# Half-length rows for the second tile's loads and the first store in an fp32 interleave kernel

## The chip, the cores and the metric

The kernel runs on 1 core of one Trainium2 chip. The metric is the device time of one execution in microseconds (us). I call the two versions "the kernel before" and "the changed kernel". The span in a profile runs from the first to the last instruction that the profile shows. Spans are compared with spans and times with times.

## The reference

```python
# x, y: (32, 256, 1024) float32
result = np.zeros((32, 256, 2048), dtype=np.float32)
result[..., 0::2] = x
result[..., 1::2] = y
```

It is pure data movement: 67.1 MB are read and 67.1 MB written.

## The kernel before

Inputs and output are taken as flat arrays. Eight tiles of 128 partitions x 8192 elements are loaded from x and from y, so a partition's row is 32 KiB. VectorE interleaves each tile in two halves into an output tile of 128 x 8192, whose row is 32 KiB as well. Loads are issued from SyncE (queue q1), stores from ScalarE (queue q10). x, y and output tiles have two buffers each.

```python
WL = 8192; WS = 4096
xpool = ...(name="xp", bufs=2); ypool = ...(name="yp", bufs=2); opool = ...(name="op", bufs=2)
...
nc.scalar.dma_start(out=first, in_=zero)      # a small store of zeros at the very start
for lw in lwidths:                            # 8 tiles
    ...
    nc.sync.dma_start(out=xtile, in_=xs)
    nc.sync.dma_start(out=ytile, in_=ys)
    while soff < lw:                          # 2 halves
        otile = opool.tile([P, 2 * WS], fp32, name="otile")
        ...
        nc.vector.tensor_copy(out=otile[:, 0::2], in_=xsub)
        nc.vector.tensor_copy(out=otile[:, 1::2], in_=ysub)
        nc.scalar.dma_start(out=os_, in_=otile)
```

## Time and profile before

| what | value | from |
|---|---|---|
| time, median of the first 3 runs | 316.41 us (315.72 to 316.87) | runs |
| span of the profiled run, whose time is 315.62 us | 313.8 us | page, first line; runs |
| VectorE busy | 23% | page, part 1 |
| both DMA queues together | 99.4% of the 16 engines' time | page, part 3 |
| moved | 428 GB/s over the span, 433 from 31 to 311 us | page; stretches |

The page is read from the DMA parts. The share of a queue says how long its packets took, as a part of 16 engines times the span. Two shares that add up to almost 100% leave no room for any gain but shorter or fewer packets. Numbers are taken from the packet records (start, length and size of every row that an engine moved). The text of the prediction shows the other views.

### The profile page before, as it was taken

Reading aid. Unit: us, or ns where it says so; the run is one execution under the profiler, and the core shown is the slowest. Engines: PE = TensorE matmul, PEld = TensorE weight load, DVE = VectorE, ACT = ScalarE, POOL = GpSimd, SP = SyncE. Lnnn points to the kernel's source line nnn. Section 1 sums busy time; section 2 is a strip of 40 time slices with the busy share of each in tenths; the row PEclk is TensorE's granted clock in tenths of the full one; section 3 lists DMA queues with packets and bytes.
Section 4 is the critical chain, followed back from the end, with each engine's and each line's share of the span. In section 5 each row is a group of like instructions: output and inputs, shape, how many; then the busy total and the mean of one; then the engine's idle time right before and its main releaser. Section 6 shows DMA issues by size and latency. Waiting matters only on the chain.

```text
span 313.8 us, 152 instructions
## 1 busy us (share of the span) xinstructions
DVE 72.8 (23%) x33; POOL 0.2 (0%) x4
## 2 busy tenths in 40 slices
DVE  0433002231032410325003150130501305023500
POOL 0000000000000000000000000000000000000000
DMA  8999999999999999999999999999999999999997
GB/s 339 464 405 397 468 401 464 405 464 405 464 405 464 405 459 409 451 418 451 418 434 434 430 439 426 443 413 455 401 468 401 468 401 468 401 468 401 464 405 334
DMA packets 4640, 134.23 MB, mean 428 GB/s; under 512 B 528, under 2 KB 544, under 8 KB 544
## 3 DMA queue, kind: packets, MB, share of 16 engines
q1 hardware_dynamic: 2304, 67.11, 49.9%
q10 hardware_dynamic: 2336, 67.12, 49.5%
HBM read 67.11 MB, written 67.12 MB: 428 GB/s over the span
## 4 chain that ended last, share of the span: by engine, by line
DMA 83%; DVE 11%; DVEq 1%; issue 0%
DMA out_dram<-otile 76%; DMA ytile<-in_y_dram 7%; DVE otile L71 6%; DVE otile L70 5%; DVEq L83 1%; DVEq L70 0%
## 5 line engine op out<-in xcount | busy, mean ns | idle before, releaser
L70 DVE COPY otile<-xtile 128x4096 f32<-128x4096 f32 x16 | 36.6, 2295 | 184.9 <-DMA out_dram<-otile 173.7
L71 DVE COPY otile<-ytile 128x4096 f32<-128x4096 f32 x16 | 36.6, 2292 | 39.8 <-DMA ytile<-in_y_dram 39.8
L45 DVE MEMSET zero<- 16x128 f32 x1 | 0.2, 165 | 0.9 <-PEq L119 0.9
L119 POOL MEMSET const-bfloat16-1.0<- 128x1 bf16 x1 | 0.1, 102 | 0.0
L119 POOL MEMSET const-uint8-127<- 128x1 uint8 x1 | 0.1, 102 | 0.0
L119 POOL MEMSET const-float32-0.0<- 128x1 f32 x1 | 0.1, 99 | 0.2 <-issue 0.2
L119 POOL MEMSET const-float32-1.0<- 128x1 f32 x1 | 0.1, 99 | 0.0
## 6 DMA issues: line engine op xcount, KB each, us to landing
out_dram<-otile ACTq DMA_DIRECT2D x16, 4096.0 KB, 29.1
xtile<-in_x_dram SPq DMA_DIRECT2D x8, 4096.0 KB, 43.6
ytile<-in_y_dram SPq DMA_DIRECT2D x8, 4096.0 KB, 60.7
out_dram<-zero ACTq DMA_DIRECT2D x1, 8.0 KB, 6.3
```

Source lines behind the costliest of these rows:

```text
L45: nc.vector.memset(zero, 0.0)
L70: nc.vector.tensor_copy(out=otile[:, 0::2], in_=xsub)
L71: nc.vector.tensor_copy(out=otile[:, 1::2], in_=ysub)
L83: tc.compile()
L119: nc = _bacc.Bacc("TRN2", target_bir_lowering=False, num_devices=1)
```

## The change

The second tile's x and y loads, and the first store, are each issued as two transfers of half a row (16 KiB) in every partition. Bytes and copies stay the same. The intent that I read from it is to let the first tiles get moving in smaller steps: the first copies of tile two need only the first halves, and a queue that gets the engine for one row at a time holds it for a shorter time. (The cut below is shortened; its last call is broken over fewer lines than in the kernel.)

```diff
-        nc.sync.dma_start(out=xtile, in_=xs)
-        nc.sync.dma_start(out=ytile, in_=ys)
+        parts = 2 if start == P * lw else 1
+        for t, s in ((xtile, xs), (ytile, ys)):
+            step = lw // parts
+            for c in range(0, lw, step):
+                nc.sync.dma_start(
+                    out=t[:, c : c + step],
+                    in_=dataclasses.replace(s, offset=start + c, ap=[[lw, P], [1, step]]),
+                )
...
-            nc.scalar.dma_start(out=os_, in_=otile)
+            step = width if start == 0 and soff == 0 else 2 * width
+            for c in range(0, 2 * width, step):
+                nc.scalar.dma_start(
+                    out=dataclasses.replace(os_, offset=2 * start + 2 * soff + c,
+                                            ap=[[2 * lw, P], [1, step]]),
+                    in_=otile[:, c : c + step],
+                )
```

More of the change, by code (lines that the diff above doesn't have):

```diff
@@ L71, in _interleave @@
             nc.vector.tensor_copy(out=otile[:, 1::2], in_=ysub)
-            nc.scalar.dma_start(out=os_, in_=otile)
+            step = width if start == 0 and soff == 0 else 2 * width
+            for c in range(0, 2 * width, step):
+                nc.scalar.dma_start(
+                    out=dataclasses.replace(
+                        os_,
+                        offset=2 * start + 2 * soff + c,
+                        ap=[[2 * lw, P], [1, step]],
+                    ),
+                    in_=otile[:, c : c + step],
+                )
             soff += width
```

## The prediction

> **What bounds the kernel now.** I read the page's header, its DMA parts and its chain first, because the kernel does no arithmetic: it reads 67.11 MB, interleaves, and writes 67.12 MB.
>
> ```profile
> span 313.8 us, 152 instructions
> DVE 72.8 (23%) x33; POOL 0.2 (0%) x4
> ...
> DMA packets 4640, 134.23 MB, mean 428 GB/s; under 512 B 528, under 2 KB 544, under 8 KB 544
> q1 hardware_dynamic: 2304, 67.11, 49.9%
> q10 hardware_dynamic: 2336, 67.12, 49.5%
> ...
> DMA 83%; DVE 11%; DVEq 1%; issue 0%
> ```
>
> The two queues (q1 the loads, q10 the stores) together fill 99.4% of the 16 engines' time. Of q1's 2304 packets, 256 are 4-byte completions (16 for each of 16 loads), so 2048 are rows of 32 KiB, 128 on each engine; q10 has as many. 49.9% of 313.8 is 156.6 us, or 1.223 us a row; 49.5% is 155.3 us, or 1.213 us a row. In the packet records nearly every row takes exactly 1.213 us. So the floor is 256 rows per engine x 1.213 = 310.5 us, only 3.3 us (1.05%) under the span. VectorE, at 23%, is no bound.
>
> Next, where those 3.3 us are. I asked for stretches of the span (columns: DVE and POOL busy, clock, DMA share, GB/s):
>
> ```profile
> 1.00:22.00 21.00, 4.53 (x4) 0.00 (x0) 1.00 1.01 423
> 24.00:31.00 7.00, 2.50 (x2) 0.00 (x0) 1.00 0.97 379
> 31.00:311.00 280.00, 63.61 (x28) 0.00 (x0) 1.00 1.00 433
> ```
>
> From 31 to 311 us nothing is lost: 433 GB/s for 280 us. The losses are three. The start: the first row begins at 0.99 us, and first rows take about 2.0 us in place of 1.213 (together about 1.7 us). The entry of the stores: the 16 load rows that begin near 27.3 us, just ahead of the first store rows, take 1.69 to 1.88 us, about 0.57 us too long on every engine. The end: the last row ends near 312.7 us and the last store lands at about 313.1, about 1 us for the landing and the closing. Only the second lies in what the change touches.
>
> Third, the waits and the tail, because the change moves when buffers come free:
>
> ```profile
> DVE otile L70 <- DMA out_dram<-otile: 173.7, 14, 21.6
> DVE otile L71 <- DMA ytile<-in_y_dram: 39.8, 8, 5.2
> DVE otile L70 <- DMA xtile<-in_x_dram: 11.3, 1, 11.3
> ```
>
> ```profile
> 287.67 2.29 DVE L71 COPY otile<-ytile 128x4096 f32<-128x4096 f32 x1 [4.92 <-DMA ytile<-in_y_dram]
> 290.00 8.66 ACTq L72 DMA_DIRECT2D out_dram<-otile  x2
> 293.80 2.30 DVE L70 COPY otile<-xtile 128x4096 f32<-128x4096 f32 x1 [3.83 <-DMA out_dram<-otile]
> ```
>
> VectorE's 225 us of waiting is for DMA that is itself busy: consequences, not costs. The tail matters. The last load lands at 287.65 us. The store then in flight lands at 293.70, so 6.05 us, that is 5 rows, of it are left. In those 5 rows VectorE copies the last y (2.29 us), the next store is issued at 290.00, and the engines never run dry.
>
> **What the Trainium skill says.** The page "DMA: Bandwidth & Descriptors", section "Queues, rings and completion order", says that each engine round-robins between the queues with work, a packet at a time. The trace agrees, with one 32 KiB row as the turn: from 30 us on the packet records show 16 load rows, 16 store rows, in strict alternation. So a queue's share goes by the size of its rows, and this is the lever of the change. The same page, section "Where 436 GB/s comes from", puts the ceiling at 435 GB/s; the trace shows 433, so there is 0.5% of head room. Its section "Why small descriptors are slow (HBM only)" charges a fixed overhead per packet. The records let me size it: 27 ns for a 512-byte row and 1213 ns for 32 KiB, a line with 1186 / 32256 ns per byte and about 8 ns fixed. "Perfetto Trace Analysis", section "DMA Optimizations", says that splitting lets some transfers start sooner if the DMA engines are generally idle; here they are not.
>
> **The change, part by part.** The instruction order shows the same copies on VectorE, four loads of half rows in place of two for the second tile (x first half, x second, y first, y second), two half-row stores in place of the first one, and nothing else but which completion semaphores are shared.
>
> 1. *Rows.* Two loads and one store get 256 half rows each in place of 128 rows: 384 more packets, 24 per engine. By the line above a half row takes 0.61 us, so 24 x 8 ns = 0.2 us, on the bound. Three more completions per engine at 9 ns are 0.03 us. Sum: +0.2 us.
>
> 2. *Entry of the stores.* The first store is issued at 24.32 us and its first rows begin at 29.10: 4.8 us, in which load rows already taken up by the engines run out. If the engines hold a count of rows, half rows shorten this toward 2.4 us, and may halve the 0.57 us of slow load rows. I take -0.3 us, the only term that can gain. The earlier start itself gains nothing, as loads fill the engines anyway.
>
> 3. *The lead of the loads over the stores.* Before, it settles near 21 rows and stays, as both queues alternate row for row. While the first store (half rows) meets the second tile (half rows), shares stay equal: after 8 rows of store, about 29 of load are done (28 if the stores enter earlier), with 3 to 4 rows of y left. Then the second store has full rows against half rows and gets two thirds: it moves 6 to 8 rows while the loads move 3 to 4. The lead falls to 17 or 18 rows. From then on rows are equal again.
>
> 4. *What the smaller lead does.* Each even store (the first half of a tile) needs its y landed. With lead 21, 5 rows of the odd store are left at that moment, and between loads and stores they last 12 us (94.05 to 106.20 us in the timeline). With lead 18, 2 rows are left, lasting 4 x 1.213 = 4.9 us; the copy takes 2.3 us and the entry of a store up to 4.8, together 7.1. The store queue would run dry for about 2 us. But loads are queued behind, so the engines don't stop: they do 2 more load rows, and the lead climbs to some 19 or 20 by itself. Cost: perhaps one more slow entry of 0.57 us, which I count half: +0.3 us.
>
> 5. *Tail.* With lead 19 to 20, 3 to 4 rows (3.6 to 4.9 us) of the last odd store remain when the last y lands. Copy 2.3 us plus issue and start of about 1.0 us (first load: issued at 0.00, first row at 0.99) is 3.3, so little or nothing is lost. With lead 17 it would be 3.3 + 0.8 of a slow first row - 1.2 = 2.9 us. Weighing these, +0.3 us.
>
> 6. *Other waits.* The second half of y1 shares a semaphore with the small zero store, landed by 7.4 us; the third y load now waits for the first half store, landing near 37 us by my reckoning, while some 7 rows of loads are still queued. Both hidden: 0. The y split lets the first copy of tile two start without all of y1, which takes away a wait of 4.9 us at 55.32 us on VectorE; hidden as well: 0.
>
> Sum: 0.2 - 0.3 + 0.3 + 0.3 = +0.5 us on 316.4, which gives 316.9 us.
>
> **The rivals.** *The tail opens:* the lead doesn't recover and the engines stand still before the last two stores. For it: the 2:1 share is a plain consequence of turns by rows. Against: loads stay queued behind, which restores the lead. It would make 318 to 320 us. *The entry becomes smooth:* half rows remove the slow 0.57 us and nothing else happens. For it: the loss sits exactly where the change works. Against: it is all there is to win, and 0.2 us go back in rows. It would make 316.0 us. *Half rows are badly slower than my line,* for instance by 0.1 us each through a change of HBM access: the 48 half rows per engine would cost 5 us, giving 321. Against: 512-byte rows lie on the engine's line, and all big rows take the same 1.213 us for reads and writes. *Nothing but noise:* 316.4 us, within the 1.15 us between the three runs of before.
>
> **Range and chances.** The best case is -0.6 us less noise, about 315.3; the tail at a middling size gives 318.6. Faster by over 2% would need under 310.1 us; the rows alone take 310.5, so this is all but excluded: 1%. Slower by over 2% needs over 322.7 us, more than full tail loss and a second slow entry together: 2%. Within 2%: 97%.
>
> **What would show it.** Right: the DMA share stays near 1.00 from 31 to 311 us; packets rise by 384 + 48 completions; first store rows before 29.1 us and shorter slow rows there; the second store lands sooner than 67.4 us, by about 3 us; at the end the last y lands later and fewer than 5 rows of the store in flight are left. Wrong: a gap in the DMA row near 290 us, half rows that take clearly over 0.61 us, or a lead that stays at 21, which would mean that turns go by bytes rather than rows. The prediction fails if the time is below 315.3 (something hidden in the 280 us was gained) or above 318.6.

## The result, and the profile after

The changed kernel took 316.62 us (median of 6 runs, 316.54 to 316.93), the kernel before beside it 316.15 us (315.67 to 316.87). Ratios here are the mean time of one kernel's fast runs over that of the other's of the same rounds, so not quite the ratio of the medians. This one is 1.0015 (95% interval 1.000 to 1.003): the same at 2%, some 0.5 us longer. The interval reaches 1.000; the repeat in experiment 8 is clear of it (1.0007 to 1.0033).

The page of the changed kernel, in the lines that answer to those of before:

```profile
span 314.5 us, 159 instructions
...
DMA packets 5072, 134.23 MB, mean 427 GB/s; under 512 B 576, under 2 KB 592, under 8 KB 592
q1 hardware_dynamic: 2592, 67.11, 49.9%
q10 hardware_dynamic: 2480, 67.12, 49.5%
```

There are 432 packets more, the 384 half rows and the 48 completions of the working. The shares are what they were: the engines are as full as before, in a span 0.7 us longer (of which some 0.5 us are the fast run that was profiled before). In the packet records a half row takes 611 ns, as worked out.

The stretches of the changed kernel (columns as in the prediction):

```profile
1.00:22.00 21.00, 4.68 (x4) 0.00 (x0) 1.00 1.01 423
24.00:31.00 7.00, 2.34 (x2) 0.00 (x0) 1.00 1.00 382
31.00:311.00 280.00, 63.52 (x28) 0.00 (x0) 1.00 1.00 433
```

The start is equal, the entry of the stores is hardly better (382 GB/s for 379) and the long middle is at 433 GB/s in both. What did move is the order of things. First the timeline of the kernel before from 48 to 70 us, then that of the changed kernel (columns: start, length, engine, line, operation, tiles; in brackets the idle time before it and what ended it):

```profile
48.11 2.29 DVE L70 COPY otile<-xtile 128x4096 f32<-128x4096 f32 x1 [21.62 <-DMA out_dram<-otile]
55.32 2.30 DVE L71 COPY otile<-ytile 128x4096 f32<-128x4096 f32 x1 [4.91 <-DMA ytile<-in_y_dram]
...
67.49 2.30 DVE L70 COPY otile<-xtile 128x4096 f32<-128x4096 f32 x1 [9.88 <-DMA out_dram<-otile]
```

```profile
48.75 2.29 DVE L78 COPY otile<-xtile 128x4096 f32<-128x4096 f32 x1 [22.41 <-DMA out_dram<-otile]
50.95 2.29 DVE L79 COPY otile<-ytile 128x4096 f32<-128x4096 f32 x1
...
65.16 2.30 DVE L78 COPY otile<-xtile 128x4096 f32<-128x4096 f32 x1 [11.92 <-issue]
...
84.69 2.30 DVE L78 COPY otile<-xtile 128x4096 f32<-128x4096 f32 x1 [15.03 <-DMA out_dram<-otile]
97.75 2.29 DVE L79 COPY otile<-ytile 128x4096 f32<-128x4096 f32 x1 [10.77 <-DMA ytile<-in_y_dram]
104.05 2.30 DVE L78 COPY otile<-xtile 128x4096 f32<-128x4096 f32 x1 [4.00 <-DMA out_dram<-otile]
```

The wait for y1 at 55.32 us is gone, and the second store lands 2.3 us sooner: the copy that it releases starts at 65.16 us instead of 67.49. Its full rows met half rows and got about two thirds (71% of the bytes moved from 49.5 to 57 us). The price shows at 97.75 us: the loads are later against the stores, VectorE waits 10.8 us for y (5.0 before), and the next store lands only 4.0 us after that copy (9.9 before).

The end of the changed kernel, to be laid beside the same lines in the prediction:

```profile
290.35 2.30 DVE L79 COPY otile<-ytile 128x4096 f32<-128x4096 f32 x1 [8.74 <-DMA ytile<-in_y_dram]
292.68 6.26 ACTq L82 DMA_DIRECT2D out_dram<-otile  x2
294.07 2.30 DVE L78 COPY otile<-xtile 128x4096 f32<-128x4096 f32 x1 [1.43 <-DMA out_dram<-otile]
```

The last y lands at 290.33 us, 2.7 us later than before, and the store in flight lands at 293.98. So 3.65 us of it are left, where 6.05 were left before. The copy and the start of the next store don't fit into them. The stretch from 292 to 296 us, first before, then changed, shows the hole (second to last column: the DMA share; last: GB/s):

```profile
292.00:296.00 4.00, 2.21 (x1) 0.00 (x0) 1.00 0.93 401
```

```profile
292.00:296.00 4.00, 2.58 (x2) 0.00 (x0) 1.00 0.87 369
```

A short stretch is noisy (in the kernel before the DMA share is 1.48 from 26 to 28 us and 0.61 from 28 to 30), so I also chained the rows of each engine by their ends and starts (the records don't name the engine). In the changed kernel 16 rows end from 293.07 to 293.62 us, and the next 16 start from 293.52 to 293.67: all engines but one stand still, for 0.1 to 0.6 us. In the repeat (experiment 8) up to four go on without a stop.

### The profile page after: what moved, and what is told of

The parts are those of the page before. It is cut to its first block, busy times and chain, and to the rows that moved or that the text cites. A ratio compares the mean times of both kernels' runs of the same rounds, so it can differ in the third digit from the quotient of the medians.

```text
span 314.5 us, 159 instructions
## 1 busy us (share of the span) xinstructions
DVE 72.7 (23%) x33; POOL 0.2 (0%) x4
## 3 DMA queue, kind: packets, MB, share of 16 engines
q10 hardware_dynamic: 2480, 67.12, 49.5%
## 4 chain that ended last, share of the span: by engine, by line
DMA 79%; DVE 11%; issue 4%; DVEq 1%
DMA out_dram<-otile 73%; DMA ytile<-in_y_dram 7%; DVE otile L79 6%; DVE otile L78 5%; DVEq L100 1%; DVEq L78 0%
```

## The experiments

Two theories stood against each other. **Tail theory:** the smaller lead of the loads over the stores opens the hole near 293.6 us, and this is most of the 0.5 us. **Entry theory:** the hole only makes early engines wait for late ones, and what counts is the slowest engine, made later by the half rows themselves and by slow load rows where stores enter the queues (near 27 us). All outputs were correct. Experiments 1 to 4, 5 to 8 and 9 to 11 share their runs of the kernel before (medians 316.22, 315.98 and 315.75 us), and each of these sets ran on a chip of its own (2, 8 and 11); between sets, compare through the kernel before. Neither theory looks outside the DMA; the section on the prediction shows that most of the 0.5 us lies there, and corrects the readings of experiments 1, 5, 6 and 7 for it.

### 1. The second store in half rows too

```diff
-            step = width if start == 0 and soff == 0 else 2 * width
+            step = width if start == 0 else 2 * width
```

> Undoes the unequal share alone: the second store goes in half rows too, so it meets the half rows of y1 on equal terms. Lead theory (the small loss is mostly the tail, through the lead of loads over stores): the second store lands after 67 us as before, the lead stays near 21 rows, about 5 rows (6 us) of the store in flight are left when the last y lands, no gap near 290 us, time 0.3 us over before (the rows and the slow entry), so below the changed kernel. Rival (the loss is the rows and the entry, the tail costs nothing): time 0.5 to 0.6 us over before, no faster than the changed kernel, as there are 8 more rows per engine.

Measured: 316.83 us, ratio 1.0022 (1.0004 to 1.004). The end of its timeline:

```profile
284.76 2.30 DVE L78 COPY otile<-xtile 128x4096 f32<-128x4096 f32 x1 [10.02 <-issue]
286.97 2.29 DVE L79 COPY otile<-ytile 128x4096 f32<-128x4096 f32 x1
289.29 10.03 ACTq L82 DMA_DIRECT2D out_dram<-otile  x2
294.45 2.29 DVE L78 COPY otile<-xtile 128x4096 f32<-128x4096 f32 x1 [5.20 <-DMA out_dram<-otile]
```

The last y landed at 284.68 us, 9.7 us before the store in flight landed. The lead was even over that of before (about 26 rows, not 21): the second store in half rows outlasts y1 and then meets full rows of x2, which I had overlooked. There is no hole, and still the time is not below the changed kernel's. This speaks for the rival, but weakly: the tail theory's 0.3 us over before (a ratio of 1.0009) lies within the interval, and 0.15 us more of its time than of the changed kernel's lie outside the span (table below).

### 2. The first store in half rows, all loads in full rows

```diff
-        parts = 2 if start == P * lw else 1
+        parts = 1
```

> Only the first store in half rows, all loads in full rows. If turns go by rows, the loads get two thirds while the first store runs: it lands near 58 us instead of 48, the lead rises from 21 to about 29 rows, and at the last y some 13 rows (over 12 us) of stores are left, so no tail gap. Time: before plus 0.1 us. If turns go by bytes, the first store lands near 48 us as before. For the entry: if half rows of the store make it slow, the excess near 28 us is over the 0.6 us of before; if it is the loads' rows, it stays at 0.6.

Measured: 316.04 us, ratio 0.9998 (0.998 to 1.0017). The copy that waits for the first store shows when it landed:

```profile
59.30 2.29 DVE L78 COPY otile<-xtile 128x4096 f32<-128x4096 f32 x1 [32.68 <-DMA out_dram<-otile]
```

It landed 11.2 us later than before (59.30 against 48.11), as expected from turns by rows. At the last y, 9.7 us of store were left (landings at 284.34 and 294.02 us), somewhat less than I expected. The slow load rows at the entry came to about 0.95 us per engine, in two rows of each engine, against 0.64 before. The time shows nothing of it. The spans of its runs are even shorter than those of the kernel before (314.17 against 314.52 us on average), but the ranges overlap.

### 3. Only the loads of the second tile in half rows

```diff
-            step = width if start == 0 and soff == 0 else 2 * width
+            step = 2 * width
```

> Only the second tile's loads in half rows. By rows as turns, the first store gets two thirds and lands near 42 us instead of 48. The lead falls to about 16, the store queue runs dry once or twice while loads fill the engines, and the lead comes back to 20 or more by that. Lead theory: if it is back at 20 or more at the end, there is no gap near 290 us, and the time is before plus 0.2 to 0.4 us (rows and entry); if each new entry of the stores costs 0.6 us again, before plus 0.8 to 1.4 us. Rival (lead stays where the start put it): about 0 rows left at the last y, a gap of 3 us, before plus 3 us.

Measured: 317.37 us (median of the five fast runs), ratio 1.0029 (1.0011 to 1.0047); one run of the six, 324.45 us, was slow and is left out of both. That is 0.9 to 1.15 us over before, in the range forecast for the case that each new entry of the stores costs 0.6 us again; but the slow rows after 60 us come to only 0.12 us per engine on average. Its timeline in two places:

```profile
45.40 2.30 DVE L78 COPY otile<-xtile 128x4096 f32<-128x4096 f32 x1 [18.87 <-DMA out_dram<-otile]
...
101.85 2.30 DVE L79 COPY otile<-ytile 128x4096 f32<-128x4096 f32 x1 [13.34 <-DMA ytile<-in_y_dram]
104.06 2.29 DVE L78 COPY otile<-xtile 128x4096 f32<-128x4096 f32 x1
...
289.45 2.29 DVE L79 COPY otile<-ytile 128x4096 f32<-128x4096 f32 x1 [4.88 <-DMA ytile<-in_y_dram]
```

The first store was ahead (45.40 us). At 104.06 us VectorE went on without any wait: the store before had long landed, so the store queue had run dry (no store row runs from 97.6 to 107.7 us). Counted from the packet records the lead was 14.8 rows at 60 us and 21.7 at 120 us. At the last y (289.42 us) 6.1 us of store were left, as before. So the lead comes back by itself, and this kernel has no hole at the end either, but it is the slower one. Its engines end 1.9 us apart (312.54 to 314.48 us; before 312.27 to 312.70), with 8 slow rows between 60 and 284 us, where the kernel before has none. Here, then, a slowest engine does end late.

### 4. Quarter rows in place of half rows

```diff
-        parts = 2 if start == P * lw else 1
+        parts = 4 if start == P * lw else 1
-            step = width if start == 0 and soff == 0 else 2 * width
+            step = width // 2 if start == 0 and soff == 0 else 2 * width
```

> The same change with 8 KiB rows (four parts instead of two), so 4:1 instead of 2:1 against the second store, and 72 extra rows per engine instead of 24. Lead theory with recovery: the lead falls to about 12, the store queue runs dry for some 10 us early on while loads run alone, and the lead jumps to about 22, so the tail has 5 or 6 rows left and no gap: only rows (72 x 5 to 8 ns = 0.4 to 0.6 us) and at most one more slow entry (0.6): before plus 0.5 to 1.2 us. Rival without recovery: the stores end with no rows left at the last y, a gap of 4 us or more, before plus 4 to 5 us.

Measured: 316.91 us, ratio 1.0036 (1.0003 to 1.0068; one run of 319.75 us pulls the mean up). The lead fell to 13.4 rows at 80 us and was 20 to 22 from 120 us on; 4.8 us of store, 4 rows, were left at the last y, one row less than forecast. The recovery that I predicted holds under a disturbance twice as strong, and the cost is in the foreseen range.

### 5 and 6. Half rows for x1 or y1 alone

```diff
+            parts = 2 if start == P * lw and t is xtile else 1     # 5; 6 has: t is ytile
```

> The change with y of the second tile left in full rows: only x1 and the first store are in half rows. x1 is what runs when the first store enters (near 27 us). y1 in full rows meets the half rows of the first store, so loads gain and the tail has over 5 rows left: no tail gap. Entry theory (the half rows of x1 at the entry make the slowest engine later; the first experiment lost its tail gap without getting faster): 0.3 to 0.7 us over before. Tail theory: within 0.2 us of before.

> The change with x of the second tile left in full rows: only y1 and the first store are in half rows. The entry of the stores happens beside full rows of x1, as in the kernel with the store alone. x1 in full rows against the half store lets loads gain about 4 rows, y1 in half rows against the second store loses some: the lead ends near 21 to 24 and the tail has no gap. Entry theory: within 0.2 us of before. Rival (any half rows of loads cost, wherever they run): 0.3 to 0.7 us over before, as with x1 alone.

Measured: x alone 316.23 us, ratio 1.0006 (0.9993 to 1.0019); y alone 316.25 us, ratio 1.0008 (0.9994 to 1.0021). Neither kernel had a hole at the end. The entry theory in its narrow form, that the half rows of x1 running beside the entry do the harm, expected 0.3 us or more for x alone and is not borne out, though the interval (up to 0.6 us) doesn't exclude it. Each costs some 0.2 us, not clear of zero, and none of it lies in the span: the medians of the spans are 314.2 us for both and for the kernel before.

### 7. The hole at the end closed

```diff
-            nc.vector.tensor_copy(out=otile[:, 1::2], in_=ysub)
+            half = width // 2 if start == 7 * P * lw and soff == 0 else width
+            for h in range(0, width, half):
+                nc.vector.tensor_copy(out=otile[:, 2 * h + 1 : 2 * (h + half) : 2],
+                                      in_=ysub[:, h : h + half])
-            step = width if start == 0 and soff == 0 else 2 * width
+            step = width if start in (0, 7 * P * lw) and soff == 0 else 2 * width
```

> The changed kernel, and in the last tile the y copy for its first store and that store in two column halves, so that the store can start 1.15 us earlier after the last y. This closes the gap of about 0.4 us per engine near 293.6 us and touches nothing before 290 us. Tail theory: 0.4 us faster than the changed kernel (0.1 us over before). Entry theory (the gap only lets the earlier engines wait for the later ones, two engines had no gap at all): at most 0.15 us faster than the changed kernel, so 0.3 to 0.5 us over before, with the engines ending more spread than before.

Measured: 316.75 us, ratio 1.0027 (1.001 to 1.0043). The stretch that showed the hole:

```profile
292.00:296.00 4.00, 2.65 (x2) 0.00 (x0) 1.00 0.98 422
```

The hole is closed, and the kernel isn't faster than the changed one in the same rounds (experiment 8). In the chained records the engines now end at 312.58 to 313.20 us, on average 0.27 us sooner than in the changed kernel (312.99 to 313.15), but the last one ends at the same time. So the hole is real, and closing it gains nothing that these runs resolve, where the tail theory had forecast 0.4 us.

### 8. The changed kernel again

> The changed kernel unaltered, beside the three above on the same chip, to see how far its own value moves from one set of rounds to the next. Expected 0.3 to 0.7 us over before; slow load rows at the entry, a gap near 293.6 us in most engines.

Measured: 316.63 us, ratio 1.002 (1.0007 to 1.0033). The changed kernel repeats to 0.01 us in the median; the kernel before moved from 316.22 to 315.75 us between sets. Here the engines without a stop at 293.6 us were, where I could tell them apart, those with a slow load row near 64 us (87 to 252 ns too long).

### 9 and 10. The last tile's y copy done twice

```diff
             nc.vector.tensor_copy(out=otile[:, 1::2], in_=ysub)
+            if start == 7 * P * lw and soff == 0:
+                nc.vector.tensor_copy(out=otile[:, 1::2], in_=ysub)
```

> The kernel before with the y copy for the first store of the last tile done twice: the store is issued 2.3 us later. Measures the slack of the tail before. From the trace: last y at 287.65 us, two copies of 2.3 us, issue and start 1.0 us: 293.3 us, and the store in flight ends its rows near 293.2. So the delay is hidden: 0 to 0.5 us over before. If the slack of 5 rows were not real: 2.3 us.

> The same doubled copy in the changed kernel, which has 3.65 us left at the last y instead of 6.05 and spends them all. Lead theory: nothing hides the 2.3 us, so 2.0 to 2.4 us over the changed kernel (2.5 to 2.9 over before). If the changed kernel still had slack: under 1 us.

Measured: in the kernel before 316.02 us, ratio 1.0007 (0.9993 to 1.0021); in the changed kernel 319.0 us, ratio 1.0105 (1.0091 to 1.0118). The same stretch of the latter:

```profile
292.00:296.00 4.00, 3.97 (x3) 0.00 (x0) 1.00 0.50 213
```

The same 2.3 us are hidden before, but for 0.3 us, and in the changed kernel they cost 2.4 us (319.0 against the 316.63 of experiment 8) or, through the kernel before of each set, 2.6 us. Over the kernel before it is 3.3 us, above the 2.5 to 2.9 that I forecast. The change has used up the slack of the tail. In the changed kernel the last landing comes 23.18 us after that of the last y (290.33 to 313.51); with the doubled copy 25.52 us (290.22 to 315.74), one copy more. In the kernel before 23.18 us after the last y would be 310.8, and the real last landing is 313.06, so 2.2 us were free.

### 11. Half rows everywhere

```diff
-        parts = 2 if start == P * lw else 1
+        parts = 2
-            step = width if start == 0 and soff == 0 else 2 * width
+            step = width
```

> Every load and every store in half rows: 256 extra rows per engine instead of 24. Measures the row term by itself. From the pitch of rows in the changed kernel (two half rows 1.214 us, a full row 1.209) 5 ns for each extra row: 1.3 us; by the durations (2 x 611 against 1213) 9 ns: 2.3 us. With the entry near 0.5 us: 1.5 to 3.0 us over before. If half rows were free, 0.5 us.

Measured: 317.39 us, ratio 1.0053 (1.0039 to 1.0067). All 4096 rows are cut:

```profile
DMA packets 9249, 134.24 MB, mean 425 GB/s; under 512 B 1040, under 2 KB 1056, under 8 KB 1056
```

0.53% of 315.8 us is 1.7 us for 256 extra rows per engine, 6.5 ns each if all of it is theirs. (The slow first rows and the entry together are as before in its records, 1.31 against 1.34 us per engine, and so are the other two parts of the table below.) For the 24 extra rows of the change that is at most 0.16 us.

## Why the prediction was right, step by step

The time was forecast as 316.9 us and was 316.62; a rise of 0.5 us was forecast, and 0.5 and 0.65 us (316.63 against 315.98) were found. The class and the size came out, but the size by luck: most of the rise is none of the four terms of the sum.

**Where the 0.5 us are.** Two numbers that I had overlooked show it. The first is time minus span, which each run lists: this part of the time lies before the first or after the last instruction of the profile. The second is the time from the last landing to the end of the span. After the last landing SyncE goes through its waits for the completion semaphores that are left. In the kernel before none is left (landing 313.06 us, next step 313.12); in the changed kernel three are, 0.06 us apart (landing 313.51 us, next step 313.76), though each takes only 28 ns, so that what it waits for is there already. The differences in the table are to the kernel before of the same rounds, by means:

| kernel | time minus span, us | last landing to end, us | time over before, us | of it left for the DMA, us |
|---|---|---|---|---|
| before | 1.79 | 0.79 | | |
| changed; again (8) | 2.05; 2.04 | 0.98; 0.98 | 0.48; 0.64 | 0.03; 0.19 |
| 1, both stores | 2.20 | 1.01 | 0.68 | 0.05 |
| 2, store only | 2.08 | 0.85 | -0.06 | -0.42 |
| 3, loads only | 1.79 | 0.92 | 0.92 | 0.80 |
| 4, quarter rows | 1.94 | 0.85 | 1.03 | 0.82 |
| 5, x; 6, y | 2.03; 2.05 | 0.92; 0.92 | 0.21; 0.27 | -0.16; -0.13 |
| 7, hole closed | 2.17 | 1.00 | 0.84 | 0.24 |
| 9, copy twice, before | 1.76 | 0.79 | 0.20 | 0.23 |
| 10, copy twice, changed | 2.07 | 0.98 | 3.29 | 2.81 |
| 11, all half | 1.78 | 0.79 | 1.63 | 1.64 |

The first two columns are sharp: time minus span is 1.75 to 1.83 us in 31 runs before and 2.02 to 2.08 in 11 runs of the changed kernel; the second column is one profile each, but it is 0.79 in the kernel before and in experiment 9, which has the same transfers, and 0.98 in all three profiles with the transfers of the change. So 0.26 us of the rise lie outside the span and 0.19 us in the closing waits, 0.45 of the 0.5 to 0.65 us. The last column has the noise of the runs (standard errors of 0.1 to 0.5 us). The part outside the span comes with extra stores: extra loads alone don't raise it (experiment 3), nor does cutting every store (experiment 11). Its cause isn't known, and no run was made to separate it.

**The failed statement.** The prediction put the landing and the closing at about 1 us and said that of the three losses only the entry lies in what the change touches. The closing was touched (0.19 us). The waits for shared semaphores were looked at in step 6 and set at 0, but only while the loads ran, not at the end.

**Step 1, rows:** right. A half row takes 611 ns, and experiment 11 limits the term to 0.16 us. One argument for it was circular: the 512-byte rows "lie on the line" because it was drawn through them. The half rows and the 8 KiB rows of experiment 4 (309 ns) do test it.

**Step 2, entry of the stores:** wrong. I had expected 0.3 us less. From its issue to its first rows the first store took 4.3 us (24.17 to 28.50) instead of 4.8, and the slow load rows added up to 0.75 us per engine against 0.64 before. In the repeat they were 0.64, and in experiment 9, whose entry is that of the kernel before, 0.75. So this term is zero within its scatter of about 0.1 us.

**Steps 3 and 4, the lead:** right. The packet records give a lead of about 21 rows before; in the changed kernel 17.1 at 60 us and 18 to 20 later on. Experiments 3 and 4 push it down to 13 to 15 rows, and it comes back to about 20 or more by the store queue running dry while loads fill the engines. The cost of coming back was booked as 0.3 us; in the records it is a slow row in a few engines, 0.03 to 0.06 us on average.

**Step 5, tail:** the mechanism was right, the accounting wrong. 3.65 us of store were left, at the low end of the 3.6 to 4.9 forecast, the hole is there (a gap near 290 us was one of the prediction's own signs of being wrong), and the slack is gone (experiments 9 and 10). But the 0.3 us were added to a sum in which they don't add: with the hole closed the time stays (experiment 7). Of that kernel's time, 0.15 us more than of the changed kernel's lie outside the span and in the closing waits, and with that taken off the two are equal within the noise. Two bounds lie side by side, the path from the last y (last landing at 313.51 us) and the work of the slowest engine (313.55 us with the hole closed).

**Step 6, the other waits:** right for those that it names. The removed wait for y1 at 55.32 us was worth nothing.

So the terms measured are at most 0.16 us of rows, 0 at the entry, 0.03 to 0.06 for the lead and about 0 for the tail. Their sum is about 0.2 us. The gain that failed to come and the costs booked too high cancelled in part, and 0.45 us outside the sum made up for the rest.

**What stays open:** why the part outside the span grows with extra stores; that the order of the closing waits follows from the extra transfers is my reading, not tested. What is left for the DMA, 0 to 0.2 us, is not told apart from the rows and the noise. Experiment 3 is slower by 0.8 us on the DMA engines themselves, one of which ends late; why it does so is not settled. A version that beats both kernels wasn't found.

## What to carry to other kernels

Where the DMA engines are full from end to end, count rows first: bytes over the rate of a full row give a floor, and a change that moves no bytes can win only what lies above it. Row length is then a lever on who goes first, since each queue gets one row in turn; check what the shifted order does to the slack at the end, and whether it is set right again on the way. A hole in the trace is worth nothing until closing it moves the end: try that before booking it. And before you look for half a microsecond among the rows, compare two simple differences, time minus span and last landing to end; here they held most of it.

## What the Trainium skill lacked or had wrong

- "DMA: Bandwidth & Descriptors", section "Queues, rings and completion order", describes the turn of a queue as a packet of several descriptors. For rows of 32 or 16 KiB here the turn is a single row, which the trace calls a packet (it doesn't show descriptors): in the packet records load and store rows alternate one by one for most of the time, and half rows in the loads let a store in full rows land at 45.4 us instead of 48.1 (experiment 3), half rows in the store at 59.3 us (experiment 2).
- The same page, section "Why small descriptors are slow (HBM only)", gives the overhead of a packet in cycles and for small sizes. For large rows the records show 27 ns for 512 B, 611 ns for 16 KiB and 1213 ns for 32 KiB, so about 8 ns fixed; at most 6.5 ns of it per extra row reach the time (experiment 11).
- The same page, section "Where 436 GB/s comes from", from which the prediction takes the ceiling of 435 GB/s, also says that for transfers between HBM and SBUF the HBM side, about 358 GB/s, is what binds. Here 433 GB/s were moved, loads and stores together, for 280 us.
- No page that I read has the cost of a store queue's entry beside running loads: rows of load just ahead of the first store take 1.7 to 1.9 us instead of 1.213 us, about 0.6 us on every engine, and the first store row starts 4.8 us after the issue (kernel before).
- No page that I read says how far apart the 16 engines complete one load: within 0.6 us of each other in the kernel before, and 3.2 us apart for the last y of experiment 3 (286.26 to 289.42 us).
- No page that I read says what one more transfer costs after the last landing: 0.19 us more to the end of the span and 0.26 us more outside it, in the changed kernel.
